# RWKV-7 main part of a hybrid decoder layer: the next group's inverse product and value transpose between the state steps, and finished projection blocks handled by kinds of operation behind the copies of px

## The chip, the cores and the metric

One core of one Trainium2 chip. The metric is device time in microseconds (us) of the whole program, lower is better. A profiled execution is told with two numbers: its time, and its span from the first to the last instruction of the program.

## The reference

One layer (sequence 1024, width 1024, fp32) of a trunk that mixes three heads groups in parallel (HGRN2, a dilated window attention, RWKV-7), followed by a gated MLP with a causal convolution, a per-layer embedding and a last norm. The change touches the RWKV-7 part alone, with 4 heads of 64 columns, and the input projection whose blocks are computed beside it:

```python
z = rmsnorm(h, norm_mix_g[l]) @ w_in[l]
a_q, a_f, a_i, a_g, b_q, b_k, b_v, c_in = jnp.split(z, splits, axis=-1)
...
def rwkv7_mix(c, ...):
    ...
    def step(state, inp):
        r_t, w_t, k_t, v_t, kk_t, a_t = inp
        sa = jnp.einsum('bhvk,bhk->bhv', state, -kk_t)
        state = (state * w_t[:, :, None, :] + sa[..., None] * (kk_t * a_t)[:, :, None, :]
                 + v_t[..., None] * k_t[:, :, None, :])
        return state, jnp.einsum('bhvk,bhk->bhv', state, r_t)
    _, y = lax.scan(step, s0, xs)
    mean = jnp.mean(y, axis=-1, keepdims=True)
    var = jnp.mean((y - mean) ** 2, axis=-1, keepdims=True)
    y = ((y - mean) * lax.rsqrt(var + RK_GN_EPS)).reshape(B_, S_, RK_WIDTH) * ln_w + ln_b
    ...
```

## The kernel before

The input projection has blocks of 128 columns by 1024 tokens. A block is 8 row tiles of `x`, each with three fp32r products (weight high part with `x` high and low, weight low part with `x` high; lines 130, 132, 134), for two halves of 512 tokens. Its sums lie in a PSUM tile `dp` of two banks; there are two such tiles. Four more banks are the pool `mx`, one bank to a tile, for everything else of the RWKV part.

RWKV runs over two head pairs, `p` = 0 and 1. For each pair: preparation, an inverse of 32x32 blocks on VectorE (DVE) with projection blocks on TensorE (PE) under it, and then the main part (`rwkv_groups`), which works through 16 chunks of 64 tokens in four groups of four. Here the order of PE, DVE, ScalarE (ACT) and GpSimd (POOL) is the order in which the program writes it (`manual_schedule`). SyncE (SP) and everything traced outside such a stretch is ordered by the planner of the framework, which puts instructions in by its own costs, between the written ones too. DMAs of weights and of finished blocks are issued from SP.

In the main part the projection is the filler: `fill(k)` issues k steps of a generator (`project_steps`), each step being the three products of one row tile and one half. A block has 16 steps, and three blocks are handed to each pair: 14, 15 and 24 to p=0, and 21, 22 and 27 to p=1. When the last step of a block is issued, its finishing is left in `self.pend["z"]`, and `self.pending("z")` issues it. Finishing (`project_done`, `finish`) multiplies the sums by the factor `R` of the norm, and by the kind of the block does more; the result `zst` goes to DRAM:

- kind 2: one DVE product with R out of PSUM (L470), nothing else
- kinds 0, 1 and 3: a scaling in place in PSUM on DVE (L306), a sigmoid on ACT (L473), and for 1 and 3 a DVE product of the two (L475)
- for kinds 0 to 2 of blocks under 24 the time axis is reversed, and the block is finished in two parts of 512

Block 14 is of kind 2, 15 of kind 3 (in one part of 1024), 21 of kind 1, 22, 24 and 27 of kind 2. The last projection blocks ahead of the main parts are 13 (kind 1) and 20 (kind 0).

One group before the change, in the written order (PE unless named; tile names as in the profile):

1. finish a waiting block; parts of the output norm of the first half (`rwkv_norm_in`, parts 0 and 3)
2. `pt` transposes of v; fill 1; inverse product `py` from `AB` and `T` (L860), ACT copy to `Y` (L861), POOL `scores_bd` of the next group (L801)
3. ACT places the v transposes into `XV` (L828, four copies); transposes of `ar`, placed into `Xr` (four copies); `sc` products (L871), masked by DVE into `AK` and `W` (L785); fill 1
4. `pu` from `U` and `Y` (L882), DVE `copy_predicated` into U (L883); transposes of bhat and khat (L821), placed by DVE into `PB` and by ACT into W; DVE `quad("T")` of the next group (L794); POOL copies into W; fill 1
5. `pk` (L896), ACT copy into Xr; fill 2; `px` (L901); ACT and DVE copies to `X` (L903), ACT copies to XV (L905); fill 2
6. `pgm` (L909), DVE adds into `GM` (L913, four instructions in two pairs); `pn` (L922), DVE `N`; weight split of the next block (`self.pending("w")`: ACT casts L106, POOL subtractions L108); fill 1
7. four state steps u = 0 to 3: `pS` from GM and S (L939), DVE `S` (L940), output products into `pyo` (L942, L944); a fill behind u = 0
8. DVE `quad("U")` of the next group; ACT copies pyo into y (L954, four copies)

A tile of the pool `mx` is taken again once all its readers are done.

Of the kernel before, what the change touches and what calls it, by code (L numbers as in the profile page):

```python
# [10 lines left out]
F32 = mybir.dt.float32  # L11
F32R = mybir.dt.float32r
U8 = mybir.dt.uint8
AF = mybir.ActivationFunctionType
ALU = mybir.AluOpType
# [3 lines left out]
P = 128  # L19
T = 1024  # L20
# [59 lines left out]
class Trunk:  # L80
# [375 lines left out]
    def project_done(self, j, ps):  # L456
        t = self.keep.tile([P, T], F32, tag="zst", name=self.nm("zst"), bufs=2)
        kind = (j - 8) % 4 if j < 24 else 2
        parts = [(t, ps, self.R)]
        if j < 24 and kind < 3:  # L460
            parts = [(t[:, :HT], ps[:, HT:][:, ::-1], self.R[:, HT:][:, ::-1]), (t[:, HT:], ps[:, :HT], self.R[:, :HT])]
        for part in parts:
            self.finish(kind, *part)
        d = self.zpool.tile([P, T], F32, tag=f"z{j}", name=f"z{j}")
        self.nc.sync.dma_start(d, t)
        self.z[j] = d
# [299 lines left out]
    def rwkv_groups(self, p, rp, d, y3, steps):  # L766

        nc, mxp = self.nc, self.mxp
        ar, v, gC = d["ar"], d["v"], d["gC"]
# [3 lines left out]
        def rt(name, shape, bufs=1):  # L773
            return rp.tile(shape, F32, tag=name, name=self.nm(name), bufs=bufs)

        def fill(k):
            for _ in range(k):
                next(steps)
# [8 lines left out]
        t = {}  # L787
# [11 lines left out]
        def scores_bd(g):  # L799
            t["AB", g] = w = rt("ABt", [P, 4, P])  # L800
            nc.gpsimd.tensor_tensor(w.rearrange("p u (h i) -> p u h i", i=64),  # L801
                                    d["sc"][:, group(g), :].unsqueeze(2).broadcast_to([P, 4, 2, 64]),
                                    msk[:, 0, :, :].unsqueeze(1).broadcast_to([P, 4, 2, 64]), ALU.mult)
# [14 lines left out]
        def turn(src):  # L818
            pt = mxp.tile([P, 2, P], F32, tag="mx", name=self.nm("pt"))
            for b in (0, 1):  # L820
                nc.tensor.transpose(pt[:, b, :], src(b), self.ident)  # L821
            return pt

        def place(pt, dst, copy, swap=0):
            for h, q in enumerate(Q):
                d4 = dst(h).rearrange("p (b two) v -> p b two v", two=2)
                for c in (0, 1):
                    copy(d4[Q[h ^ swap], :, c, :], pt[64 * c:64 * c + 64, :, q])  # L828
# [3 lines left out]
        W, XV = rt("W", [P, 4, 2, 2, 64]), rt("XV", [P, 4, 2, 64])  # L832
# [8 lines left out]
        quad("T", 0)  # L841
        quad("U", 0)
        add_ar(0)
        S = None
        for g in range(4):
            cs, last = group(g), g == 3
            c2 = lambda b: slice(4 * g + 2 * b, 4 * g + 2 * b + 2)
            t2 = lambda b: slice(256 * g + P * b, 256 * g + P * b + P)
            Xr = rt("xr", [P, 4, P])
            self.pending("z")  # L850
            if g == 2:
                self.rwkv_norm_in(p, d, 0, (0,))
            if last:
                self.rwkv_norm_in(p, d, 0, (3,))
            pv = turn(lambda b: v[:, t2(b)])
            fill(1)
            Y = rt("Y", [P, 4, P])
            py = mxp.tile([P, 4, P], F32, tag="mx", name=self.nm("py"))
            for u in range(4):
                nc.tensor.matmul(py[:, u, :], t["AB", g][:, u, :], t["T", g][:, u, :], start=True, stop=True)  # L860
            nc.scalar.copy(Y, py)  # L861
            if not last:
                scores_bd(g + 1)
            place(pv, lambda h: XV[:, :, h, :], nc.scalar.copy, 1)
            place(turn(lambda b: ar[:, c2(b), 0, :].rearrange("p c i -> p (c i)")), lambda h: Xr[:, :, 0:64], nc.scalar.copy)
            if g == 2:
                self.rwkv_norm_in(p, d, 0, (1,))
            ps = mxp.tile([P, 4, 2, 64], F32, tag="mx", name=self.nm("sc"))
            kbf = t["kb"].rearrange("p c a b -> p c (a b)")
            for u in range(4):  # L870
# [8 lines left out]
            U = t["U", g]  # L879
# [6 lines left out]
                quad("T", g + 1)  # L886
            for h, q in enumerate(Q):
                nc.gpsimd.tensor_copy(W[q, :, h, :, :], PB[q])
            if g == 2:
                self.rwkv_norm_in(p, d, 0, (2,))  # L890
            place(turn(lambda b: d["kh"][:, t2(b)]), lambda h: W[:, :, h, 1, :], nc.scalar.copy, 1)
            fill(1)
            pk = mxp.tile([P, 4, 64], F32, tag="mx", name=self.nm("pk"))
            for u in range(4):
# [8 lines left out]
                copy(X[q, :, q], px[q, :, 0:64])  # L903
            for h, q in enumerate(Q):
                nc.scalar.copy(XV[q, :, h, :], px[q, :, 64:128])  # L905
            fill(2)
            pg = mxp.tile([P, 4, 2, 64], F32, tag="mx", name=self.nm("pgm"))
            for u in range(4):
# [20 lines left out]
            py = mxp.tile([P, 4, 64], F32, tag="mx", name=self.nm("pyo"))  # L929
            for u in range(4):  # L930
# [14 lines left out]
                S = Sn  # L945
                if u == 0:
                    fill(1)
            if not last:
                quad("U", g + 1)
            y4 = y3.rearrange("p (b h) v -> p b h v", h=2)  # L950
            py4 = py.rearrange("p (b two) v -> p b two v", two=2)
            for h in (0, 1):
                for c in (0, 1):
                    nc.scalar.copy(y4[64 * c:64 * c + 64, 2 * g:2 * g + 2, h, :], py4[64 * h:64 * h + 64, :, c, :])  # L954


    def hgrn_setup(self):
# [938 lines left out]
```

## Time and profile before

| what | us |
|---|---|
| median of 3 runs | 1458.14 (1458.09 to 1458.71) |
| profiled execution | 1458.02 |
| its span | 1456.2 |
| PE busy in the span | 1427.3 |
| DVE, ACT, POOL busy | 1102.3, 635.3, 447.3 |
| main part of p=0 (four groups) | 146.28 to 215.13 |
| main part of p=1 (four groups) | 334.30 to 403.39 |

The times in a row of the timeline are the start and the length in us, then engine, line of the kernel, operation, output and inputs, and in brackets the idle time of the engine just before and what ended it. Rows of several equal instructions are merged (x2, x4). PEld is the weight load of PE, which overlaps its products. An fp32 product is two passes and counts twice.

### The profile page before, as it was taken

The page shows a single profiled execution, that of the slowest core. Times are in us where ns is not written, and L with a number is a line of the kernel's source. Part 1 is how long each engine was busy: PE and PEld are TensorE (multiplying, and loading weights), DVE is VectorE, ACT ScalarE, POOL GpSimd, SP SyncE. Part 2 cuts the span into 40 slices and gives each one's busy share as a digit, 9 for nine tenths or more (in the row PEclk, how much of TensorE's full clock was granted, in tenths as well). Part 3 has the DMA queues.
Part 4 walks back from the last instruction along what each step waited for, and adds up shares of the span by engine and source line. Part 5 has one row for each costly group of instructions (what it writes and reads, how often), then busy time and mean ns, then how long its engine had stood idle before and what let it go on. Part 6 is the DMA issues. An engine that isn't in the chain of part 4 may idle for free.

```text
span 1456.2 us, 20345 instructions
## 1 busy us (share of the span) xinstructions
PE 1427.3 (98%) x7480; PEld 1174.8 (81%) x7480; DVE 1102.3 (76%) x1672; ACT 635.3 (44%) x1131; POOL 447.3 (31%) x364
## 2 busy tenths in 40 slices
PE   9999999999999999899999999999999999999996
PEld 7888887888877777788878888888888888888885
DVE  6567565684677689637798889888888799777685
ACT  6531443213434565335544434444444444455552
POOL 2332342223421132222145545544454000002342
PEclk9999999999999999999999999999999999999998
DMA  5224021240151320165423332333333883352443
GB/s 215 69 82 114 30 74 58 66 129 31 58 203 44 116 73 23 66 224 209 153 93 109 109 100 96 109 103 107 108 96 122 311 287 96 103 165 58 127 157 115
DMA packets 80019, 167.84 MB, mean 115 GB/s; under 512 B 20080, under 2 KB 22256, under 8 KB 79920
## 3 DMA queue, kind: packets, MB, share of 16 engines
q1 hardware_dynamic: 65568, 145.44, 30.2%
q10 hardware_dynamic: 13408, 17.57, 3.6%
q0 software_dynamic: 944, 3.54, 0.7%
q8 instruction: 59, 0.97, 0.3%
q14 instruction: 40, 0.33, 0.1%
HBM read 120.12 MB, written 46.40 MB: 114 GB/s over the span
## 4 chain that ended last, share of the span: by engine, by line
PE 85%; DVE 6%; issue 3%; ACT 2%; POOL 2%; DMA 2%; SPq 0%; DVEq 0%; ACTq 0%; POOLq 0%
PE bg L1351 15%; PE bv L1351 11%; PE dp L130 8%; PE dp L134 8%; PE dp L132 8%; PE bg L1669 7%; PE bv L1669 7%; PE hsc L1029 2%; PE bv L130 1%; PE bv L134 1%; PE bv L132 1%; PE bg L130 1%; PE bg L132 1%; PE bg L134 1%; PE swq L1186 1%
## 5 line engine op out<-in xcount | busy, mean ns | idle before, releaser
L130 PE MATMUL dp<-xh,whi 128*128 128x512 f32 x544 | 197.5, 408 | 1.3 <-ACT xh L375 1.3
L134 PE MATMUL dp<-xh,wlo 128*128 128x512 f32 x544 | 189.1, 393 | 0.1
L132 PE MATMUL dp<-xl,whi 128*128 128x512 f32 x544 | 188.5, 392 | 0.4 <-DVE xl L376 0.3
L108 POOL TENSOR_TENSOR wlo<-raw,whi 128x512 fp32r<-128x512 f32 x84 | 136.4, 1643 | 75.1 <-ACT whi L106 75.1
L108 POOL TENSOR_TENSOR wlo<-wraw,whi 128x512 fp32r<-128x512 f32 x63 | 89.3, 1422 | 226.8 <-ACT whi L106 208.2
L1351 PE MATMUL bg<-t,whi 128*128 128x512 f32 x352 | 132.5, 389 | 0.8 <-DVE ct L1554 0.8
L106 ACT CAST whi<-wraw 128x512 fp32r<-128x512 f32 x120 | 72.6, 617 | 129.8 <-PE dp L132 87.0
L130 PEld LDWEIGHTS dp<-xh,whi 128*128 128x128 f32 x544 | 101.6, 189 | 24.0 <-issue 3.5
L134 PEld LDWEIGHTS dp<-xh,wlo 128*128 128x128 f32 x544 | 102.3, 188 | 22.3 <-POOL wlo L108 0.5
L132 PEld LDWEIGHTS dp<-xl,whi 128*128 128x128 f32 x544 | 102.4, 189 | 20.4 <-DVE xl L376 0.6
L108 POOL TENSOR_TENSOR wlo<-s,whi 128x512 fp32r<-128x512 f32 x44 | 66.6, 1514 | 160.9 <-ACT whi L106 160.9
L1669 PE MATMUL bg<-t,whi 128*128 128x512 f32 x308 | 94.9, 389 | 0.0
L1669 PE MATMUL bv<-t,whi 128*128 128x512 f32 x308 | 94.8, 389 | 0.0
L106 ACT CAST whi<-s 128x512 fp32r<-128x512 f32 x66 | 39.0, 620 | 122.3 <-PE bg L1351 113.4
L106 ACT CAST whi<-raw 128x512 fp32r<-128x512 f32 x88 | 52.7, 619 | 90.9 <-issue 48.3
L175 POOL TENSOR_TENSOR rst<-rst,mhalf 128x4 f32<-128x4 f32 (+1 forms) x9 | 10.1, 1130 | 222.7 <-DVE rst L173 222.7
L108 DVE TENSOR_TENSOR wlo<-wraw,whi 128x512 fp32r<-128x512 f32 x57 | 47.7, 836 | 40.2 <-ACT whi L106 35.8
L1351 PEld LDWEIGHTS bg<-t,whi 128*128 128x128 f32 x352 | 66.0, 188 | 14.7 <-ACT whi L106 1.1
L1665 ACT CAST t<-t 128x512 fp32r<-128x512 f32 x77 | 47.8, 623 | 47.6 <-PE bv L1669 34.1
L1669 PEld LDWEIGHTS bv<-t,whi 128*128 128x128 f32 x308 | 57.8, 188 | 12.0
L1669 PEld LDWEIGHTS bg<-t,whi 128*128 128x128 f32 x308 | 57.7, 188 | 12.0
L1351 PE MATMUL bg<-t,wlo 128*128 128x512 f32 x176 | 67.2, 389 | 0.0
(424 smaller groups left out, 3610.6 us busy)
## 6 DMA issues: line engine op xcount, KB each, us to landing
raw<-in_ffn_up_dram SPq DMA_DIRECT2D x44, 512.0 KB, 3.7
wraw<-in_w_in_dram SPq DMA_DIRECT2D x29, 512.0 KB, 3.7
z<-zst SPq DMA_DIRECT2D x18, 512.0 KB, 2.8
gb<-ct SPq DMA_DIRECT2D x33, 256.0 KB, 2.3
t<-gb SPq DMA_DIRECT2D x33, 256.0 KB, 2.8
t<-gt SPq DMA_DIRECT2D x33, 256.0 KB, 2.7
zl<-z SPq DMA_DIRECT2D x16, 512.0 KB, 4.1
wraw<-in_ple_gate_dram SPq DMA_DIRECT2D x16, 512.0 KB, 3.6
```

The lines of the kernel that those rows point to most:

```text
L106: nc.scalar.copy(hi, src)
L108: eng.tensor_tensor(lo, src, hi.bitcast(F32), ALU.subtract)
L130: nc.tensor.matmul(ps[hf], wh, xh[hf], start=first, stop=False)
L132: nc.tensor.matmul(ps[hf], wh, xl[hf], start=False, stop=False)
L134: nc.tensor.matmul(ps[hf], wl, xh[hf], start=False, stop=last)
L175: nc.gpsimd.tensor_tensor(r2[:, :n], r[:, :n], self.mhalf[:, :n], ALU.pow)
L1029: nc.tensor.matmul(sc[:, c, :], ks[:, c * P:(c + 1) * P], view(qt, c * P, [2 * n, 64 // n], [HT + n, 2], [1, n]), start=True, stop=True)
L1186: nc.tensor.matmul(pq[h][:, b:b + w], d["q"][hs, qb * P:nk], d["k"][hs, b:b + w], start=True, stop=True)
L1351: nc.tensor.matmul(ps, w[part == 2][:, s], X[k][part == 1], start=start and k == part == 0, stop=k == 3 and part == 2, skip_group_check=no ...
L1665: nc.scalar.copy(xh, x)
L1669: nc.tensor.matmul(ps[m], wt[part == 2][:, m * P:(m + 1) * P], (xh, xl)[part == 1], start=k == part == 0, stop=k == NK - 1 and part == 2)
```

## The change

Three edits. In `project_done` blocks of kinds 0, 1 and 3 are finished operation by operation over their parts instead of part by part. In the main part the inverse product with its copy to Y, `scores_bd` and `quad("U")` of the next group move behind state step 1, and the v transposes of the next group with a fill behind step 2; those of the first group stand ahead of the loop. The copies of pyo into y move into the next group, behind the placing of `ar`; finishing a block moves behind the copies of px; the parts of the norm move with them (0 into group 2 behind the placing of khat, 1 behind the copies of px, 2 into group 3, 3 behind step 1 of group 3, with a fill).

```diff
         if j < 24 and kind < 3:
             parts = [(t[:, :HT], ps[:, HT:][:, ::-1], self.R[:, HT:][:, ::-1]), (t[:, HT:], ps[:, :HT], self.R[:, :HT])]
-        for part in parts:
-            self.finish(kind, *part)
+        if kind == 2:
+            for part in parts:
+                self.finish(kind, *part)
+        else:
+            for _, src, r in parts:
+                self.scale(src, r)
+            for dst, src, _ in parts:
+                self.nc.scalar.activation(dst, src, AF.Sigmoid)
+            if kind in (1, 3):
+                for dst, src, _ in parts:
+                    self.nc.vector.tensor_tensor(dst, dst, src, ALU.mult)
...
-        S = None
+        def inverse_first(g):
+            t["Y"] = rt("Y", [P, 4, P])
+            py = mxp.tile([P, 4, P], F32, tag="mx", name=self.nm("py"))
+            for u in range(4):
+                nc.tensor.matmul(py[:, u, :], t["AB", g][:, u, :], t["T", g][:, u, :], start=True, stop=True)
+            nc.scalar.copy(t["Y"], py)
+            if g < 3:
+                scores_bd(g + 1)
+        def values_turn(g):
+            t["pv"] = turn(lambda b: v[:, 256 * g + P * b:256 * g + P * b + P])
+        def result(g, py):
...
+        S, before = None, None
+        values_turn(0)
+        fill(1)
+        inverse_first(0)
         for g in range(4):
...
-            Xr = rt("xr", [P, 4, P])
-            self.pending("z")
-            if g == 2:
-                self.rwkv_norm_in(p, d, 0, (0,))
-            if last:
-                self.rwkv_norm_in(p, d, 0, (3,))
-            pv = turn(lambda b: v[:, t2(b)])
-            fill(1)
-            Y = rt("Y", [P, 4, P])
-            py = mxp.tile([P, 4, P], F32, tag="mx", name=self.nm("py"))
...
-            place(pv, lambda h: XV[:, :, h, :], nc.scalar.copy, 1)
+            Xr, Y = rt("xr", [P, 4, P]), t["Y"]
+            place(t["pv"], lambda h: XV[:, :, h, :], nc.scalar.copy, 1)
             place(turn(lambda b: ar[:, c2(b), 0, :].rearrange("p c i -> p (c i)")), lambda h: Xr[:, :, 0:64], nc.scalar.copy)
-            if g == 2:
-                self.rwkv_norm_in(p, d, 0, (1,))
+            if before:
+                result(*before)
...
-            if g == 2:
+            if g == 3:
                 self.rwkv_norm_in(p, d, 0, (2,))
             place(turn(lambda b: d["kh"][:, t2(b)]), lambda h: W[:, :, h, 1, :], nc.scalar.copy, 1)
+            if g == 2:
+                self.rwkv_norm_in(p, d, 0, (0,))
             fill(1)
...
                 nc.scalar.copy(XV[q, :, h, :], px[q, :, 64:128])
+            if g == 2:
+                self.rwkv_norm_in(p, d, 0, (1,))
+            self.pending("z")
             fill(2)
...
                 if u == 0:
                     fill(1)
-            if not last:
-                quad("U", g + 1)
...
+                if u == 1:
+                    if last:
+                        self.rwkv_norm_in(p, d, 0, (3,))
+                        fill(1)
+                    else:
+                        inverse_first(g + 1)
+                        quad("U", g + 1)
+                if u == 2 and not last:
+                    values_turn(g + 1)
+                    fill(1)
+            before = g, py
+        result(*before)
```

More of the change, by code (lines that the diff above doesn't have):

```diff
@@ L843, in rwkv_groups @@
         add_ar(0)
-        S = None
+        def inverse_first(g):
[9 more added lines that the diff above has]
+        def result(g, py):
+            y4 = y3.rearrange("p (b h) v -> p b h v", h=2)
+            py4 = py.rearrange("p (b two) v -> p b two v", two=2)
+            for h in (0, 1):
+                for c in (0, 1):
+                    nc.scalar.copy(y4[64 * c:64 * c + 64, 2 * g:2 * g + 2, h, :], py4[64 * h:64 * h + 64, :, c, :])
+        S, before = None, None
+        values_turn(0)
+        fill(1)
+        inverse_first(0)
         for g in range(4):
@@ L848, in rwkv_groups @@
             t2 = lambda b: slice(256 * g + P * b, 256 * g + P * b + P)
-            Xr = rt("xr", [P, 4, P])
-            self.pending("z")
-            if g == 2:
-                self.rwkv_norm_in(p, d, 0, (0,))
-            if last:
-                self.rwkv_norm_in(p, d, 0, (3,))
-            pv = turn(lambda b: v[:, t2(b)])
-            fill(1)
-            Y = rt("Y", [P, 4, P])
-            py = mxp.tile([P, 4, P], F32, tag="mx", name=self.nm("py"))
-            for u in range(4):
-                nc.tensor.matmul(py[:, u, :], t["AB", g][:, u, :], t["T", g][:, u, :], start=True, stop=True)
-            nc.scalar.copy(Y, py)
-            if not last:
-                scores_bd(g + 1)
-            place(pv, lambda h: XV[:, :, h, :], nc.scalar.copy, 1)
+            Xr, Y = rt("xr", [P, 4, P]), t["Y"]
+            place(t["pv"], lambda h: XV[:, :, h, :], nc.scalar.copy, 1)
             place(turn(lambda b: ar[:, c2(b), 0, :].rearrange("p c i -> p (c i)")), lambda h: Xr[:, :, 0:64], nc.scalar.copy)
-            if g == 2:
-                self.rwkv_norm_in(p, d, 0, (1,))
+            if before:
+                result(*before)
             ps = mxp.tile([P, 4, 2, 64], F32, tag="mx", name=self.nm("sc"))
@@ L947, in rwkv_groups @@
                     fill(1)
-            if not last:
-                quad("U", g + 1)
[L950 to L954, printed above, removed]
+                if u == 1:
[10 more added lines that the diff above has]
+        result(*before)
     def hgrn_setup(self):
```

## The prediction

> **What bounds the kernel now.** The page first: TensorE (PE) is busy nearly all of the span, so time can only come from places where it waits or is fed badly.
>
> ```profile
> span 1456.2 us, 20345 instructions
> PE 1427.3 (98%) x7480; PEld 1174.8 (81%) x7480; DVE 1102.3 (76%) x1672; ACT 635.3 (44%) x1131; POOL 447.3 (31%) x364
> ```
>
> Next the view by stretches, cut at the transposes of v, one stretch for each group: the sum over the four groups of the first head pair (p=0), then the second and third group of the second pair (p=1). After the length stand PE, PEld, DVE, ACT and POOL busy, then the granted clock, the DMA share and GB/s.
>
> ```profile
> sum 68.85, PE 68.24 PEld 57.46 DVE 42.56 ACT 30.93 POOL 28.22; mean PE 17.06 PEld 14.37 DVE 10.64 ACT 7.73 POOL 7.05
> ...
> 351.30:368.11 16.81, 16.77 (x141) 14.31 (x141) 8.03 (x21) 6.21 (x21) 5.58 (x9) 1.00 0.11 32
> 368.11:386.80 18.69, 17.26 (x141) 14.26 (x141) 13.21 (x29) 10.11 (x28) 9.89 (x12) 1.00 0.07 29
> ```
>
> A group takes some 17 us (68.85 for four); the third of p=1 takes 18.69, 1.88 more than the one before it. What the change can win lies inside these eight groups. The granted clock is 1.00. Third view, the timeline of the third group of p=1, where a finished projection block (kind 1) sits ahead of the group's own work on ACT:
>
> ```profile
> 369.47 0.60 ACT L473 ACTIVATE zst<-dp 128x512 f32<-128x512 f32 x1
> 370.10 0.69 DVE L475 TENSOR_TENSOR zst<-zst,dp 128x512 f32<-128x512 f32 x1 [0.92 <-ACT zst L473]
> 371.55 0.60 ACT L473 ACTIVATE zst<-dp 128x512 f32<-128x512 f32 x1 [1.49 <-DVE dp L306]
> 372.68 1.16 PE L882 MATMUL pu<-U,Y 128*128 128x128 f32 x8 [0.77 <-ACT Y L861]
> 373.81 0.44 PE L821 MATMUL pt<-cst,bhat 128*128 128x128 f32 x2
> 374.91 0.44 PE L821 MATMUL pt<-cst,khat 128*128 128x128 f32 x2 [0.66 <-ACT xr L828]
> ```
>
> The sigmoid stands 1.49 us for the second scaling, which itself stands behind the first product on DVE. ACT's copies of Y, XV and xr come behind it, and PE waits for Y (at pu) and for xr (at the khat transpose). An ordinary group (second of p=1) for comparison:
>
> ```profile
> 353.11 0.38 PE L821 MATMUL pt<-cst,ar 128*128 128x128 f32 x2
> 353.33 1.06 PE L871 MATMUL sc<-ar,kbd 128*128 128x128 f32 x8
> 355.82 0.38 PE L821 MATMUL pt<-cst,bhat 128*128 128x128 f32 x2
> 356.24 0.44 PE L821 MATMUL pt<-cst,khat 128*128 128x128 f32 x2
> 360.94 0.43 DVE L903 COPY X<-px 64x256 f32<-64x256 f32 x1 [2.37 <-ACT X L903]
> 361.40 0.76 ACT L905 COPY XV<-px 64x256 f32<-64x256 f32 x2 [0.49 <-DVE X L903]
> 362.83 0.86 DVE L913 TENSOR_TENSOR GM<-pgm,addend 64x256 f32<-64x256 f32 x2 [1.46 <-PE pgm L909]
> 364.06 0.33 PE L939 MATMUL pS<-S,GM 128*128 128x64 f32 x2
> 364.83 0.48 PE L130 MATMUL dp<-xh,whi 128*128 128x512 f32 x1
> 366.41 0.39 PE L939 MATMUL pS<-S,GM 128*128 128x64 f32 x2
> 366.83 0.28 DVE L940 SCALAR_TENSOR_TENSOR S<-pS,gC,N 128x64 f32<-128x64 f32 x1 [0.57 <-PE pS L939]
> 367.26 0.39 PE L939 MATMUL pS<-S,GM 128*128 128x64 f32 x2
> ```
>
> **What the change wins.** (1) The khat transpose starts 0.42 us after that of bhat, where ar to sc, the same transposes unhindered, takes 0.22: it needs the PSUM buffer that ACT frees with the copies into xr. After the change Y is copied a step earlier and the v transpose is ready, so ACT opens the group with XV (1.1 us) and xr (1.1), done about 2.15 us after the ar transpose; khat is due at 2.85. The four result copies (1.1) come behind, done at 3.25 before pk at 4.0. So 0.20 goes in five groups, and 0.88 in the third of p=1 (373.81 to 374.91 against 0.22): 1.9 us. The pyo buffer now lives into the next group; the buffers of v, ar and sc come free in the order in which pu, bhat and khat need them, so I charge nothing (if khat got pyo's: 0.4 in each of six groups, 2.4).
>
> (2) The late Y of p=1: the group's excess of 1.88 less the 0.68 already in khat: 1.2 us. With Y a step early, nothing replaces it here.
>
> (3) State steps. One followed directly by the next takes 0.85 (366.41 to 367.26), one followed by a block product 0.77 (364.06 to 364.83): 0.08 each. The change puts the inverse product (0.9 us) behind step 1 and transpose with a fill behind step 2. Thirteen such joints make 1.1. In the third group of p=0 one joint is worse, 1.05 instead of 0.77:
>
> ```profile
> 195.44 0.39 PE L939 MATMUL pS<-S,GM 128*128 128x64 f32 x2
> ...
> 196.49 0.43 PE L939 MATMUL pS<-S,GM 128*128 128x64 f32 x2
> ```
>
> With that, 0.3 more (its S stood behind a weight subtraction on DVE): 1.4 us. The inverse products, the transposes and the fills only move: PE's own time for them is the same (37 fills inside instead of 36, one fewer behind, 0.69 us that is not lost). The joint costs of the new neighbours are unseen: plus or minus 0.03 each, zero taken.
>
> Here reading the share of busy time would mislead: busy leaves 0.04 of 16.81 in the second group of p=1, 1.43 in the third and 0.61 in all of p=0, so only about 2.1 could be won there, not 4.5, and the sum below would end at 1459.4. I take the starts, since (3) shows 0.08 lost between instructions that both count as busy. [...]
>
> **What it costs.** (4) The finishing now stands, in written order, between the copies of px and GM. DVE is free there from 361.37 to 362.83, 1.46 us. Kind 2 is two products with R of 0.7 or less and fits (first block of p=0, second of p=1): nothing. The first block of p=1 is kind 1. On the ordinary group's clock: scalings 361.4 to 362.8; sigmoids 362.8 to 364.0, ACT being done with XV at 362.2 and with the square of the norm (0.63) at 362.8; products 363.4 to 364.8; GM then takes 0.86, and step 0 starts at 365.7 instead of 364.06. Behind the waiting products on DVE stand GM, N and the S of every step, and PE waits for GM with all that follows it. Cost 1.7 us.
>
> (5) The second block of p=0 is kind 3, one part of 1024, so by kinds or not it is a chain:
>
> ```profile
> 205.71 1.23 DVE L306 TENSOR_TENSOR dp<-dp,rstd 128x1024 f32<-128x1024 f32 x1 [0.32 <-PE dp L134]
> 206.97 1.03 ACT L473 ACTIVATE zst<-dp 128x1024 f32<-128x1024 f32 x1
> 207.05 0.43 DVE L903 COPY X<-px 64x256 f32<-64x256 f32 x1
> 208.03 1.22 DVE L475 TENSOR_TENSOR zst<-zst,dp 128x1024 f32<-128x1024 f32 x1 [0.55 <-ACT zst L473]
> 209.17 0.85 DVE L913 TENSOR_TENSOR GM<-pgm,addend 64x256 f32<-64x256 f32 x2
> 210.17 0.40 PE L130 MATMUL dp<-xh,whi 128*128 128x512 f32 x1
> 210.41 0.33 PE L939 MATMUL pS<-S,GM 128*128 128x64 f32 x2
> ```
>
> Today the planner starts it ahead of the X copy and nobody waits. Afterwards it starts at 207.48: 1.23 + 1.03 + 1.22 with handovers ends at 211.0, GM 0.85 later, step 0 at 211.9 instead of 210.2: 1.7 us. A product of the next head pair (210.17) shows that PE's order is filled from outside in this group; the finished block's buffer frees at 211.0, so up to 0.86 of it can be filled. Between 0.85 and 1.7 I take 1.3.
>
> (6) The first groups keep their order, but the last block before them is now finished by kinds, outside the written order:
>
> ```profile
> 335.86 0.70 DVE L306 TENSOR_TENSOR dp<-dp,rstd 128x512 f32<-128x512 f32 x1 [0.66 <-ACT zst L473]
> 339.68 0.44 PE L821 MATMUL pt<-cst,khat 128*128 128x128 f32 x2 [0.49 <-ACT xr L828]
> ```
>
> The second scaling waited for the first sigmoid, so the halves of dp count as overlapping. Then the first sigmoid must now wait for both scalings, 0.7 later; ACT had 0.47 idle ahead of Y, so xr and khat slip by some 0.25 in each first group: 0.5 us. If the halves don't hold each other, 0.35 is won twice; the bounds are -0.7 and +0.8.
>
> (7) The rest. Mean and subtraction of the norm move into the 2.37 us for which DVE waits ahead of X: two operations of 128x512, some 0.7 each as in 370.10, and between them
>
> ```profile
> L728 DVE TENSOR_SCALAR gnm<-gnm x4: 171/172/1086, 182.6 to 405.5; 128x8 f32<-128x8 f32 x4
> ```
>
> so 1.6, at the worst 2.5: hidden, or 0.1 out. The variance pair goes to the same place one group on; the norm's last scaling and the U tile, some 0.7 each, behind step 1, with a product or fill between it and the next step. All hidden; without cover each would cost its own length. On POOL scores_bd goes ahead of the next group's key copies by more than a fill, and is needed a group later. On SP the z stores are issued up to most of a group later; a weight load of later blocks that stands behind one comes later too, and has the products of the block in hand to hide it. In the later stages the planner decides anew; its largest wait there bounds what a different draw is worth, 2.1 us either way, zero taken:
>
> ```profile
> PE hsc L1029 <- DVE qt L1034: 4.6, 4, 2.1
> ```
>
> **Sum.** Won 1.9 + 1.2 + 1.4 = 4.5; lost 1.7 + 1.3 + 0.5 = 3.5; net 1.0 us. The profiled execution took 1458.02 us (span 1456.2 and 1.82 around it), the median of the runs is 1458.14. 1458.02 - 1.0 = 1457.0. About 0.2%, 2.9 us, is what a measurement of this kernel can tell from no change.
>
> **Rivals.** *The stall ahead of GM doesn't come* (chance 0.25): sigmoids and products slip in beside pgm and pn, or fills cover them. Then 4.5 less 0.5: 1454.0 (1452.8 if the first groups win 0.7 too). For it speaks that today block two of p=0 costs nothing; against it that here the order is written and GM is behind the products on DVE.
>
> *Foreign casts stretch the chain; the slower side* (0.13). The planner puts weight splits of later blocks where ACT and DVE wait, and the new chain has such holes between scaling, sigmoid and product:
>
> ```profile
> 380.81 2.18 ACT L106 CAST whi<-wraw 128x512 fp32r<-128x512 f32 x4
> 385.72 1.40 DVE L108 TENSOR_TENSOR wlo<-wraw,whi 128x512 fp32r<-128x512 f32 x1
> ```
>
> Two casts (1.1) ahead of the sigmoids and one subtraction (1.4) ahead of the products add 2.5 in (4), and 1.7 in (5) where one cast can come: 4.2, 1461.2. It decides from 1.0 us of such stretching on.
>
> *The U tile holds a state step* (0.05). Behind step 1 it runs while POOL subtracts weights; it took up to 1.57 instead of 0.7:
>
> ```profile
> 387.24 1.57 DVE L794 TENSOR_TENSOR U<-Tc,cst 128x512 f32<-128x512 f32 x1
> 384.08 4.18 POOL L108 TENSOR_TENSOR wlo<-wraw,whi 128x512 fp32r<-128x512 f32 x3
> ```
>
> Step 1's S is there 0.7 us after its pS starts; U at 1.57 ends at 2.3, step 2's S at 2.6, and step 3 wants it at 3.4 (0.77 + 0.9, 0.77 + 0.15 + 0.78): covered. Only if U sat out two subtractions (1.4 each by the second row) and then took 0.7 would that S come at 4.5, 1.1 late, in the four groups that split weights: 4.4 us, 1461.4. [...]
>
> **How the numbers follow.** Forecast 0.57, rivals 0.25, 0.13, 0.05. Its own range is 1455.0 to 1459.2, from (5), (6) and part of the later draw. The whole range, 1453.4 to 1460.4, takes in most of the first rival and the beginning of the others. Faster by over 0.2% (under 1455.2): the first rival and a little of the forecast, 0.27; slower (over 1461.0): 0.11; the rest 0.62.
>
> **What would show it.** Right: khat 0.22 behind bhat from the second groups on; step to step never below a product; third group of p=1 near 18.1, waiting at pS for GM; fourth of p=0 waiting there too. Wrong: no wait at pS for GM (first rival), casts between scaling and sigmoid (second), a wait of pS for S (third), or main parts as forecast and a different loss behind 420 us.

## The result, and the profile after

The changed kernel takes 1461.38 us, median of 12 runs (1458.63 to 1463.67), against 1458.40 (12 runs, 1458.09 to 1460.26) for the kernel before on the same chip: a ratio of 1.0019, 95% interval 1.0011 to 1.0027. It is slower by about 3 us, where 1 us less was forecast. The profiled execution took 1461.37 us (span 1459.6 and 1.8 around it), 3.35 more than the one before.

The page of the changed kernel first. The head shows almost nothing: PE is busy 2.3 us more, at the same share.

```profile
span 1459.6 us, 20343 instructions
PE 1429.6 (98%) x7480; PEld 1177.3 (81%) x7480; DVE 1103.0 (76%) x1672; ACT 634.8 (43%) x1131; POOL 450.5 (31%) x364
```

That PE is *busier* by 2.3 us with the same 7480 instructions is itself the hint that instructions became longer, not only that PE waited. The waits of PE in the changed kernel (line waited at, who released it, us in total, times, longest):

```profile
PE pS L962 <- DVE GM L936: 2.0, 1, 2.0
...
PE dp L130 <- DVE zst L472: 0.9, 1, 0.9
```

The first row is the third group of p=1, the second the fourth group of p=0; in the main parts there is only one more, 0.7 us of the khat transpose in the first group of p=0. The wait at `pu` for Y, and the waits of the khat transpose in the later groups, are gone. The rest can't be seen there. It is in the view by stretches (length; busy time of PE, PEld, DVE, ACT and POOL; then the granted clock, the DMA share and GB/s). The first two rows are the second and third group of p=1, from one transpose of ar to the next; the others are cut to the edges of what they show:

```profile
353.37:370.00 16.63, 16.63 (x142) 14.26 (x141) 7.90 (x20) 6.23 (x22) 5.63 (x8) 1.00 0.08 30
370.00:390.81 20.81, 18.86 (x145) 15.75 (x145) 14.65 (x28) 10.41 (x31) 8.48 (x10) 0.92 0.17 54
380.61:384.02 3.41, 1.46 (x11) 0.99 (x10) 3.21 (x7) 2.14 (x5) 0.53 (x1) 1.00 0.35 143
384.02:387.43 3.41, 3.41 (x16) 2.89 (x16) 2.17 (x3) 0.00 (x0) 3.30 (x4) 0.50 0.03 11
387.43:390.84 3.41, 3.41 (x30) 2.84 (x29) 2.25 (x4) 1.40 (x5) 1.23 (x1) 1.00 0.63 168
493.25:496.66 3.41, 1.63 (x13) 1.11 (x12) 1.88 (x6) 3.40 (x7) 0.00 (x0) 1.00 0.97 332
496.66:500.07 3.41, 3.41 (x17) 3.41 (x18) 0.31 (x1) 0.78 (x2) 0.00 (x0) 0.50 0.87 348
```

An ordinary group got shorter (16.63; 16.81 before). The third group of p=1 got longer, and not by its wait alone: for 3.41 us behind the wait the granted clock is 0.50, and PE, busy all through, gets 16 instruction records done where the next 3.41 us have 30. The same happens at 496.66, far behind the change; the window ahead of it holds two waits of PE, 0.69 and 1.09 us long, which the kernel before has as well (0.7 and 1.09), there at full clock. In the kernel before the clock was below 1.00 only in the first 12 us and the last 11. The timeline of the changed kernel around the wait:

```profile
377.68 0.43 DVE L923 COPY X<-px 64x256 f32<-64x256 f32 x1 [0.69 <-ACT X L923]
...
378.14 1.43 DVE L306 TENSOR_TENSOR dp<-dp,rstd 128x512 f32<-128x512 f32 x2
...
379.60 1.09 ACT L469 ACTIVATE zst<-dp 128x512 f32<-128x512 f32 x2
...
380.00 0.50 PE L130 MATMUL dp<-xh,whi 128*128 128x512 f32 x1
...
380.58 2.17 ACT L106 CAST whi<-wraw 128x512 fp32r<-128x512 f32 x4
380.72 1.28 DVE L472 TENSOR_TENSOR zst<-zst,dp 128x512 f32<-128x512 f32 x2 [1.15 <-ACT zst L469]
381.93 0.85 DVE L936 TENSOR_TENSOR GM<-pgm,addend 64x256 f32<-64x256 f32 x2
...
382.92 0.41 PE L962 MATMUL pS<-S,GM 128*128 128x64 f32 x2 [1.95 <-DVE GM L936]
...
383.77 0.56 PE L130 MATMUL dp<-xh,whi 128*128 128x512 f32 x1
...
384.55 0.63 PE L134 MATMUL dp<-xh,wlo 128*128 128x512 f32 x1
384.98 0.52 PE L962 MATMUL pS<-S,GM 128*128 128x64 f32 x2
...
385.74 1.78 DVE L803 TENSOR_TENSOR U<-Tc,cst 128x512 f32<-128x512 f32 x1
...
386.33 1.64 PE L858 MATMUL py<-T,ABt 128*128 128x128 f32 x8
...
387.80 0.33 PE L962 MATMUL pS<-S,GM 128*128 128x64 f32 x2
```

Read down: scalings, both sigmoids, both products, and only then GM; PE stands at `pS` for 1.95 us. From the fill at 380.00 to `pS` go 2.92 us, where an ordinary group has 0.80: a cost of 2.12. Then the same instructions become long: a fill product of 0.63 instead of 0.40, the inverse product 1.64 instead of 1.11. Against the second group of p=1, where the clock is 1.00, the fill takes 1.21 us to the next `pS` (383.77 to 384.98) instead of 0.78, the state step 1.35 (to 386.33) instead of 0.79, and the inverse product 1.47 (to 387.80) instead of 0.95: together 1.5 us lost. By the groups it is 1.7 (from the transpose of ar at 370.00 to the next at 390.42 are 20.42 us, 16.63 in the second group, less the 2.12). I take 1.6, a cost that the prediction did not have.

**Theory.** The finishing ahead of GM makes a stall, as forecast; the stall makes PE's clock drop to half for a stretch behind it, and the length of those instructions is the second half of the price. **Rivals.** The halved stretch is chance, or comes from something else in the new order; or the loss is in the order between the state steps itself.

### The profile page after: what moved, and what is told of

It is laid out like the page before. It is cut to its first block, busy times and chain, and to the rows that moved or that the text cites. A ratio compares the mean times of both kernels' runs of the same rounds, so it can differ in the third digit from the quotient of the medians.

```text
span 1459.6 us, 20343 instructions
## 1 busy us (share of the span) xinstructions
PE 1429.6 (98%) x7480; PEld 1177.3 (81%) x7480; DVE 1103.0 (76%) x1672; ACT 634.8 (43%) x1131; POOL 450.5 (31%) x364
## 4 chain that ended last, share of the span: by engine, by line
PE 85%; DVE 6%; issue 3%; ACT 2%; DMA 2%; POOL 2%; SPq 0%; DVEq 0%; ACTq 0%; POOLq 0%
PE bg L1379 15%; PE bv L1379 11%; PE dp L130 8%; PE dp L134 8%; PE dp L132 8%; PE bg L1697 7%; PE bv L1697 7%; PE hsc L1057 1%; PE bv L130 1%; PE bv L134 1%; PE bv L132 1%; PE bg L130 1%; PE bg L134 1%; PE bg L132 1%; PE swq L1214 1%
```

## Experiments

All runs are in five rounds, beside the kernel before on the same chip. None leaves out any of the computation.

**Each part alone.** The first kernel is the one before with finishing by kinds of operation, at its old place. The second is the changed kernel with finishing part by part, at the head of the group.

```diff
 # kinds only (on the kernel before), in project_done
-        for part in parts:
-            self.finish(kind, *part)
+        if kind == 2: ...                  # scalings, then sigmoids, then products
 # main order only (on the changed kernel): project_done as before, and
+            self.pending("z")
             place(t["pv"], lambda h: XV[:, :, h, :], nc.scalar.copy, 1)
...
-            self.pending("z")
             fill(2)
```

> The kernel before with the first edit alone: blocks of kinds 0, 1 and 3 finished operation by operation over their parts; the main part stands as before. Theory A (the loss is the wait of step 0 for GM, and a stretch of halved clock that it brings): no such wait here, nothing halved that was not halved before; in the third group of p=1 the finishing stands at the head of the group as before, so pu and khat still wait, by a bit more or less; 1457.5 to 1459.0, the same as before. Theory B (the loss comes from the grouping by kinds itself, or from what the planner makes of the finished blocks outside the main parts): 1460 to 1461.5, as the changed kernel.

> The changed kernel with the finishing part by part again and at the head of the group, ahead of the placing of v; the inverse product, the v transposes and the result copies stay between the state steps. Theory A: GM is on time in the fourth group of p=0 and the third of p=1, pS waits for it no more. But in the third group of p=1 ACT does both sigmoids (the second behind the first product on DVE, about 2.7 us from the group's start) ahead of XV and xr, so xr ends near 4.9 us instead of 2.15 and khat, due at 2.85, waits 2 us: that stall takes the place of the other, with the same chance of a halved clock. 1459.5 to 1461.5. Theory B (grouping by kinds): without it the time falls to about 1455.5. Theory C (it is the interleaving of the state steps that costs): as theory A in time, but without a wait as long as 1.5 us anywhere in the main parts.

Kinds only: 1458.89 (11 runs), ratio 0.9996, interval 0.9987 to 1.0005, no change that can be told. Main order only: 1462.41 (11 runs), ratio 1.0019, interval 1.0011 to 1.0028, as slow as the whole change. Its timeline in the third group of p=1, and its stretches cut to the edges of the clock:

```profile
372.01 0.60 ACT L473 ACTIVATE zst<-dp 128x512 f32<-128x512 f32 x1 [1.49 <-DVE dp L306]
...
373.80 1.16 PE L892 MATMUL pu<-U,Y 128*128 128x128 f32 x8 [2.38 <-ACT XV L828]
```

```profile
372.58:375.99 3.41, 1.54 (x10) 1.17 (x10) 2.85 (x7) 3.15 (x13) 0.00 (x0) 1.00 0.37 154
375.99:379.40 3.41, 3.40 (x22) 2.54 (x23) 2.93 (x7) 1.37 (x5) 1.70 (x2) 0.50 0.00 0
```

Another wait, at another place (`pu` stands for the copies into XV, queued on ACT behind the second sigmoid; the expectation had put it at the khat transpose), and the same halved stretch behind it. So the halving is not tied to GM or to the new place of the finishing. And the two edits are no sum: with Y a step early, the old place of the finishing is worse than it was before.

**Take the stall away.** The finishing is cut in two: scalings and sigmoids behind the copies of px, products and the store behind state step 2. Once on the changed kernel, once on the order of the kernel before.

```diff
+        def rest():
             if kind in (1, 3):
                 for dst, src, _ in parts:
                     self.nc.vector.tensor_tensor(dst, dst, src, ALU.mult)
...
+        if later and kind in (1, 3):
+            self.pend["y"] = rest
+        else:
+            rest()
...
-            self.pending("z")
+            self.pending("z", later=True)
             fill(2)
...
+                if u == 2:
+                    self.pending("y")
```

> The changed kernel with the finishing cut in two: scalings and sigmoids stay behind the copies of px, the products of sigmoid and sum (kinds 1 and 3) and the store go behind state step 2. Theory A: the scalings fit into the 1.46 us that DVE has ahead of GM (two of 0.7, one of 1.23), so pS waits for GM by less than 0.3 us in both groups, no stretch around 384 us runs at half clock, and the time falls by the 2.1 us and the 0.9 us of these waits and 1.6 us of halved clock: 1456 to 1457.5, faster than before. Theory B or C: the waits go and the time stays at 1460 to 1461.5.

> The kernel before with the finishing grouped by kinds, its scalings and sigmoids behind the copies of px and its products behind state step 2, as in the two-stage version; the inverse product, the v transposes, the U tile, the norm and the result copies stay where they were before. If the interleaving with the state steps is worth only the khat waits (0.16 to 0.2 us in six groups, 1.1 us together) and the rest of the two-stage version's gain is the finishing that leaves the head of the third group of p=1 (1.9 us), then 0.9985 to 0.9993 of before, and the two-stage version stays ahead by 0.0005 to 0.001. If the interleaving is what won there: as before, 0.9995 to 1.0005. The wait of khat in ordinary groups stays at 0.42 from bhat, the state steps at 0.85 where they follow each other.

On the changed kernel: 1457.04 (11 runs, 1455.43 to 1457.59), ratio 0.9982, interval 0.9974 to 0.9991. On the order before: 1457.06 (11 runs), ratio 0.9986, interval 0.9978 to 0.9995. Both beat both kernels; the first stands 0.0037, some 5.4 us, below the changed kernel when each is taken against its own runs of before. The timeline of the first, same place:

```profile
376.79 1.43 DVE L306 TENSOR_TENSOR dp<-dp,rstd 128x512 f32<-128x512 f32 x2
...
378.26 0.86 DVE L943 TENSOR_TENSOR GM<-pgm,addend 64x256 f32<-64x256 f32 x2
378.26 1.09 ACT L469 ACTIVATE zst<-dp 128x512 f32<-128x512 f32 x2
...
379.46 0.33 PE L969 MATMUL pS<-S,GM 128*128 128x64 f32 x2
```

GM starts beside the sigmoids, 1.47 us behind the start of the scalings instead of 3.79, and `pS` has no wait. The two versions differ by the interleaving between the state steps; by their ratios that is worth 0.0004 (0.6 us), which their intervals don't tell from nothing.

**Keep the stall, fill PE.** Is the extra 1.6 us the stall's idleness? The changed kernel with eight products of 128x512 in the hole, written to the bank that `pS` then overwrites; then with four, and later with two. GM is as late as ever.

```diff
+                    if (p, g, u) == (1, 2, 0):
+                        wide = mxp.tile([P, HT], F32, tag="mx", name=self.nm("pS"))
+                        x = self.X[0][0][0]
+                        for _ in range(8):          # then range(4), range(2)
+                            nc.tensor.matmul(wide, x[:, :P], x, start=True, stop=True)
+                        pS = wide[:, :64]
...
```

> The changed kernel with eight additional products of 128x512 ahead of step 0 in the third group of p=1, whose sums are overwritten: they fill the time for which PE waited there (1.95 us by the trace, eight products at 0.23 are 1.85) and shorten no wait for GM. If the stall alone costs (plain theory A): GM comes as late as before, step 0 starts within 0.2 us of where it did, the time stays at 1461. If the idle stretch brings a halved clock besides: the stretch after 384 us runs at full clock, and the median falls by about 1.6 us to 1459.5 to 1460; the mean granted clock rises by about 0.001. If the halving has nothing to do with this wait: clock and time as in the changed kernel.

> The changed kernel with four additional products instead of eight ahead of step 0 in the third group of p=1, so that some 1.0 us of the 1.95 stays idle. If a halved stretch needs an idle time of well over 1 us: no halving behind it, 0.9997 to 1.0006 of before, as with eight products. If 1 us is enough: 1.0015 to 1.002, as the changed kernel. In between (1.0006 to 1.0015) if it comes in part of the runs.

> The changed kernel with two products of 128x512 in the hole instead of four: idle time of PE at pS about 1.4 us (1.95 without, 0.94 with four). Theory, sharpened from the profiles so far (the clock is judged in windows of 3.41 us on a fixed grid, and the next window is halved where PE is idle for more than about half of one, 1.6 to 1.8 us): no halved stretch behind this stall, wherever the grid lies, and a ratio near that with four, 1.0000 to 1.0008. Rival (any stall between 0.94 and 1.95 us can set it off, the bound lies nearer 1 us): a halved stretch within 4 us behind the stall, ratio 1.0011 to 1.0020. Rival (the grid doesn't matter, halving is chance in every window): halving in some profile or none, ratio between 1.0008 and 1.0016. In both theories the profile's other halved stretches lie whole multiples of 3.413 us from each other, and each follows a window with more than 1.6 us idle by the first one only.

Eight: 1459.07 (11 runs), ratio 1.0001, interval 0.9992 to 1.0009. Four: 1459.27 (11 runs), ratio 1.0003, interval 0.9994 to 1.0012. Two: 1462.22 (11 runs), ratio 1.0014, interval 1.0005 to 1.0023. The timeline with four, and the stretch behind the wait:

```profile
382.81 0.43 PE L969 MATMUL pS<-S,GM 128*128 128x64 f32 x2 [0.94 <-DVE GM L936]
```

```profile
384.00:388.00 4.00, 4.00 (x32) 3.19 (x30) 3.45 (x5) 0.84 (x2) 3.89 (x4) 1.00 0.02 9
```

and with two, where PE waits 1.40 us at `pS`, the window around the end of the wait and the two behind it:

```profile
381.95:385.36 3.41, 2.32 (x18) 1.86 (x19) 2.77 (x9) 1.01 (x2) 1.03 (x2) 1.00 0.37 154
385.36:388.78 3.42, 3.42 (x19) 3.19 (x20) 3.02 (x3) 0.59 (x1) 3.42 (x3) 0.50 0.06 11
388.78:392.19 3.41, 3.41 (x16) 2.89 (x17) 0.28 (x1) 0.97 (x4) 0.53 (x1) 0.50 0.73 240
```

With four, `pS` starts at 382.81 (382.92 in the changed kernel), so the wait for GM costs what it cost; only PE's idleness is cut, from 1.95 to 0.94 us. The clock stays at 1.00, at this place with eight products too (that profile, at 1462.51 the slowest of the eleven runs, has two halved stretches far behind, at 594.95 and 670.04), and the kernel is faster than the changed one by 0.0016 (0.0018 with eight), some 2.5 us. PE does *more* work in less time. With two the halved stretch is there, and most of the gain is gone. So the ratio follows the idleness that is left: 1.0001, 1.0003 (0.94 us), 1.0014 (1.40 us), 1.0019 (1.95 us), at the same lateness of GM. The intervals of neighbouring values overlap, those of eight products and of none do not. The granted clock that is listed with each run says the same: its mean is 0.9936 over the twelve runs of the changed kernel, 0.9940 with two products, 0.9954 with four and 0.9955 with eight. That shows that idleness makes the second half of the price. The sharpened expectation for two products, that only a window idle for more than about half its length sets the halving off, is refuted: 1.40 us of waiting did it, with 1.09 us of idleness in the window ahead of the halved one, and for two stretches at that. Of the rivals written there, the one with the bound between 0.94 and 1.40 us for such a stall stands. The ratio would also fit the third rival, that halving is chance in every window; against it, the starts of the two places in that profile, 385.36 and 596.99, are 62.0 times 3.413 us apart, where 3.413 is a 33rd of the 112.64 us between the two starts in the changed kernel. The halving doesn't come in every execution either: two of the eleven runs with two products, 1459.01 and 1459.24, have a mean clock of 0.997 and the others at most 0.994, and of the changed kernel's twelve the one at 1458.63 has 0.997.

The filling wins 2.5 and not the 1.6 us of one stretch. By the mean clocks that is still the clock: 0.0018 more of some 1460 us is 2.6 us, an estimate that takes PE as the limit all through. So the average run of the changed kernel loses more than its profile shows at this place, as the profile with two products does, which has two stretches there.

**A longer stall at the same place.** The changed kernel with finishing part by part, at the new place: the chain gets longer by what doing both scalings and both sigmoids together had saved.

```diff
 # in project_done of the changed kernel
-        if kind == 2: ...                  # scalings, then sigmoids, then products
+        for part in parts:
+            self.finish(kind, *part)
```

> The changed kernel with the first edit undone: the finishing stands behind the copies of px, but part by part. In the third group of p=1 DVE then does scaling, waits for the sigmoid, product, scaling, waits, product: 0.7 + 0.6 + 0.7 twice with handovers, 4.2 us instead of 3.5 ahead of GM. If the grouping shortens the stall: pS waits for GM by 2.6 to 2.9 us instead of 1.95, halved clock behind it as before or longer, 1.0023 to 1.0035 of before. If the grouping is without effect: 1.0019 as the changed kernel.

1463.56 (5 runs), ratio 1.0034, interval 1.0022 to 1.0046. PE waits 2.9 us at `pS`, and the halved clock lasts for two stretches:

```profile
382.96:386.37 3.41, 2.17 (x10) 1.87 (x11) 2.54 (x7) 1.67 (x4) 0.96 (x2) 0.50 0.37 154
386.37:389.78 3.41, 3.41 (x17) 2.98 (x16) 2.14 (x3) 0.00 (x0) 3.41 (x3) 0.50 0.15 25
```

The longer chain adds 1.0 us of waiting; by the ratios 2.2 us are added to the changed kernel's time, though the two intervals overlap.

**A stall with nothing else of the change.** The kernel before, with useless VectorE work ahead of GM in the second group of p=1, which is otherwise undisturbed. First on a new tile, then on the decay tile after its last reader.

```diff
 # behind the copies of px, in the kernel before
+            if (p, g) == (1, 1):
+                junk = rt("junk", [P, HT])
+                nc.vector.memset(junk, 0.0)
+                for _ in range(4):
+                    nc.vector.tensor_tensor(junk, junk, self.R[:, :HT], ALU.mult)
 # second kernel, instead
+                for _ in range(8):
+                    nc.vector.tensor_tensor(AK, AK, pm[:, 0, :].unsqueeze(1).broadcast_to([P, 4, 64]), ALU.mult)
```

> The kernel before with additional work on DVE in the second group of p=1, ahead of GM: a memset (0.5) and four products of 128x512 (0.7 each) on a tile that nobody reads, 3.25 us where 1.46 are free, so that pS waits for GM by about 1.8 us and nothing else changes. If such a wait costs its length: 1.0012 of before (plus 1.8 us). If it also brings a halved clock in most runs: 1.0018 to 1.0025, and a stretch of 3.4 us at half clock behind the wait in the trace, where the block products take about twice their time.

> The kernel before, with eight 64x512 products on VectorE more (the decay tile times a mask, written over the decay tile, which nothing reads any more there; nothing of the output changes) in the second group of pair 1 of the main part, ahead of the masking of S; no new tile, no other queue touched. Theory (a stall of about 2 us on TensorE costs its own length and then a stretch of halved clock that opens behind it): pS waits about 2 us for the masking there, the trace shows one stretch at 0.5 granted clock within some 4 us behind it, and the median lies 2.0 + 0.3 to 2.0 + 2 us above the kernel before, ratio 1.0016 to 1.0028. Rival (the stall costs only its length, and the clock's stretches in the changed kernel are chance): a wait of the same length, no halved stretch at that place, ratio 1.0010 to 1.0015. Rival (the changed kernel's loss is the finishing's and not the stall's): ratio below 1.0008.

The first gave 1469.11 (6 runs), ratio 1.0074, interval 1.0061 to 1.0088, and is inconclusive as a price: the new tile changed later stages too (a wait of 1.6 us at 1380.30 with a halved stretch from 1381.87, which the kernel before does not have). At the place meant, `pS` waits 2.54 us, and two halved stretches follow, from 368.11 to 374.94. The second: 1464.27 (5 runs), ratio 1.0043, interval 1.0029 to 1.0056. The eight operations took 4.46 us, 1.0 more than eight maskings of AK would (0.43 each), so the wait was longer than meant. Its timeline and its stretches:

```profile
361.45 4.46 DVE L908 TENSOR_TENSOR AKt<-AKt,pm 128x256 f32<-128x256 f32 x8
...
366.93 0.41 PE L942 MATMUL pS<-S,GM 128*128 128x64 f32 x2 [2.65 <-DVE GM L916]
```

```profile
365.25:368.66 3.41, 1.73 (x13) 1.48 (x13) 2.93 (x8) 0.00 (x0) 0.40 (x1) 1.00 0.00 0
368.66:372.07 3.41, 3.41 (x23) 2.83 (x21) 0.69 (x3) 0.00 (x0) 0.00 (x0) 0.50 0.00 0
372.07:375.48 3.41, 3.41 (x16) 3.00 (x15) 2.06 (x4) 1.64 (x5) 0.00 (x0) 0.50 0.00 0
```

The expected ratio (1.0016 to 1.0028) is missed on the high side, because the stall was 2.65 us and not 2.0 and was followed by two halved stretches. The kind of outcome is that of the theory: this kernel has neither the new order nor the new finishing, and the clock halves behind the stall. In place it costs 5.9 us: from the transpose of ar at 353.15 to the one at 375.85 are 22.70 us, against 353.11 to 369.93, 16.82, in the kernel before. That is 2.65 of waiting and 3.2 of slower work. In the profiled execution 1.2 of it comes back by the next stage, where the `hsc` products that began at 426.7 before begin at 431.4, 4.7 later: in the next group ACT and DVE catch up while PE is late, and the wait of 0.77 at `pu` is gone.

## Why the prediction was wrong, by its steps

Two steps failed. Step (3) counted a gain of 1.4 us that the new order doesn't have. And step (4) priced the stall ahead of GM by its length alone: the clock of 1.00 that the prediction read in the trace before was taken to stay, a term put at nothing without a reason, and it fell to 0.50 behind the stall. The stall itself came where it was forecast, and for the reason given.

Against its own net of -1.0, the profiled execution came out at +3.35. The starts of the same products in the two profiles show where. The first v transposes of p=1 are 0.97 later (335.27, before 334.30). Behind both main parts the first product `hpo` is 1.56 later (496.52, before 494.96), and behind the halved stretch at 496.66 `hsc` is 3.17 later (543.84, before 540.67); some 0.2 comes after that. So the main parts came out at +1.56 where -1.0 was forecast. The stretch at 496.66 is the draw of one execution: the waits ahead of it are not the change's.

- **(1) khat, won 1.9: right.** khat now starts 0.26 behind bhat in the second to fourth groups (356.08 and 356.34 in the second of p=1) instead of 0.42 and, in the third of p=1, 1.10. Five times 0.16 and 0.84: 1.6.
- **(2) late Y, won 1.2: right.** No wait at `pu` is left.
- **(3) joints of the state steps, won 1.4: wrong; it is about nothing.** I read the 0.08 between two state steps as something that goes when they are parted. Only the second of the two joints had it: step 1 to step 2 took 0.80 (365.61 to 366.41), step 2 to step 3 0.85. And most of it moved. The timeline of PE in the second group of p=1 before:

```profile
365.61 0.33 PE L939 MATMUL pS<-S,GM 128*128 128x64 f32 x2
...
369.04 1.05 PE L860 MATMUL py<-T,ABt 128*128 128x128 f32 x8
...
369.93 0.38 PE L821 MATMUL pt<-cst,ar 128*128 128x128 f32 x2
```

  and after the change:

```profile
364.18 0.33 PE L962 MATMUL pS<-S,GM 128*128 128x64 f32 x2
...
366.52 1.11 PE L858 MATMUL py<-T,ABt 128*128 128x128 f32 x8
367.47 0.33 PE L962 MATMUL pS<-S,GM 128*128 128x64 f32 x2
...
370.00 0.39 PE L830 MATMUL pt<-cst,ar 128*128 128x128 f32 x2
```

  From the first `pS` to the transpose of ar, with the same four steps, two fills, the v transposes and the inverse product in both kernels, are 5.82 us; before, 364.06 to 369.93, 5.87. The inverse product takes 0.95 to the next start instead of 0.89 (369.04 to 369.93 before). From ar to ar the group gains 0.19 (16.63 instead of 16.82): 0.14 ahead of the first `pS`, by khat, and 0.05 behind it, of the 0.16 forecast for its two joints. "The joint costs of the new neighbours are unseen: plus or minus 0.03 each, zero taken" is the sentence that failed: a difference between two neighbourhoods is no gain until the new neighbour has a row of its own.
- **(4) the stall ahead of GM, cost 1.7: mechanism right, sized 2.12, and its consequence missed.** The products start at 380.72, behind *both* sigmoids (379.60 for 1.09), not behind the first. That the halves of one tile count as overlapping I used in (6) and forgot here. The larger part of what was missed is the halved clock, 1.6 us. The trace before had no sign of it: its longest waits in the main parts are 0.77 and 0.66, and a longer one behind them, 2.11 us ahead of 593.58, is not followed by a halved clock there.
- **(5) the kind-3 block, cost 1.3: right, 1.1.** The timeline of the fourth group of p=0 after the change:

```profile
207.01 1.23 DVE L306 TENSOR_TENSOR dp<-dp,rstd 128x1024 f32<-128x1024 f32 x1
...
209.34 1.22 DVE L472 TENSOR_TENSOR zst<-zst,dp 128x1024 f32<-128x1024 f32 x1 [1.09 <-ACT zst L469]
...
210.71 0.70 PE L130 MATMUL dp<-xh,whi 128*128 128x512 f32 x2 [0.87 <-DVE zst L472]
...
211.71 0.33 PE L962 MATMUL pS<-S,GM 128*128 128x64 f32 x2
```

  The chain is the one written down, 0.5 earlier, and as forecast a product of the next head pair takes up a part: PE idles 0.87, then products that wait for the finished block's buffer run until GM is there. By the end of p=0 it is rather 1.2: 0.97 later there, less the 0.21 of (6), plus three times 0.16 of (1). That idle stretch trips no halving.
- **(6) first groups, cost 0.5: half right.** p=0 slipped by 0.21, as forecast. In p=1 ACT's copies into xr slipped too, by 0.2 against the group's start (339.71 for 1.08), but khat, at 340.02, no longer waits for them and came 0.63 sooner. Why it doesn't is not shown; that the gain of 0.4 lies inside the bounds given is luck.
- **(7) the rest at nothing: right for the named operations.** The norm's subtraction ends 0.69 ahead of the DVE copy of X. U took 1.78 beside POOL's subtractions, more than the 1.57 feared, and no state step waits for S behind it. What was drawn later is not a wait but a clock: at 496.66 the profiled execution loses another 1.6 us. That lies inside the 2.1 allowed, but not for the reason given.

The sum by these: won 1.6 + 1.2 + 0.4 = 3.2, lost 2.1 + 1.1 + 1.6 + 1.6 = 6.4, net +3.2 of the +3.35 measured. Without the two halved stretches it would be nothing, and there the kernels with four and eight filling products stand (1.0003, 1.0001), whose mean clocks of 0.9954 and 0.9955 are those of the kernel before. Over all runs, too, most of the loss is the clock's: 0.9936 in the changed kernel, 0.9952 to 0.9954 in the kernel before as it ran beside the experiments; the difference, 0.0016 to 0.0018 of some 1460 us, is an estimated 2.3 to 2.6 of the 3 us.

**The rivals.** "The stall ahead of GM doesn't come" did not happen. "Foreign casts stretch the chain", whose 1461.2 is by chance near the measured time, did not either: ACT's four casts (380.58) come as the sigmoids end. "The U tile holds a state step" neither. On the signs named: khat 0.26, near the 0.22 forecast, and waits were seen at both places named, in the fourth group of p=0 not at `pS` itself but at a product put in just ahead of it; "step to step never below a product" was seen and was worth nothing; "third group of p=1 near 18.1" was missed, it takes 20.4 (370.00 to 390.42), of which 1.6 by the clock.

## What to carry to other kernels

A stall on TensorE is to be priced at its length and at the slower clock that can follow it: here 1.95 us of idleness cost about 1.6 us more in the profile and 2.65 us cost 3.2 more, while a wait of 2.13 us (at 596.76 in the changed kernel) that lay across two windows was followed by none of it. So such a stall is to be avoided, or filled, with useless products if there are no others: in the profiles it was followed by full clock when filled to 0.94 us, and by half when filled to 1.40 us. Where a chain DVE, ACT, DVE stands ahead of something that PE waits for, cut it at its handovers and put the second half behind what is waited for, which here won 2 to 2.6 us against the kernel before, in either order. And a gap between two starts belongs to the pair of neighbours: when one of them is exchanged, look for the row of the new pair before counting it as won.

## What the runs showed of the hardware

- The granted clock was 0.50 in stretches of 3.41 us. In the changed kernel they begin at 384.02 and 496.66, 112.64 us or 33.0 times 3.413 apart. In all eight profiles with several such stretches behind the first 13 us and ahead of the last 20, their starts are whole numbers of 3.413 us apart (48.0 with kinds only, 62.0 with two products); the pieces of a profile counted off so from a halved stretch are its windows, and their edges its grid. One stretch followed a stall of 1.95 us (the changed kernel) and of 2.38 us (main order only); two of them, 6.82 us, followed 1.40, 2.54, 2.65 and 2.9 us; none followed 0.94, 0.87 or less in the main parts. In the changed kernel 1.95 us was enough, in a window in which PE was busy for 1.46 of 3.41 us.
- The same wait was followed by a halved stretch in one profile and by none in two others. It is the one of some 2.1 us near 592, far behind the change: in the kernel with kinds only it falls into one window (2.12 us idle), and the next window has a clock of 0.50; in the changed kernel it lies across two (1.01 and 1.12 us idle), as in the one before (2.11 us long), and the clock behind it stays at 1.00. The stretches of kinds only, then those of the changed kernel:

```profile
590.83:594.24 3.41, 1.29 (x8) 0.81 (x7) 2.73 (x3) 0.00 (x0) 1.19 (x2) 1.00 0.00 0
594.24:597.65 3.41, 3.41 (x28) 3.19 (x28) 1.30 (x2) 0.00 (x0) 0.00 (x0) 0.50 0.03 5
```

```profile
592.23:595.64 3.41, 2.40 (x12) 1.68 (x11) 2.88 (x5) 0.62 (x1) 2.03 (x2) 1.00 0.01 2
595.64:599.05 3.41, 2.29 (x30) 2.20 (x32) 2.10 (x4) 0.00 (x0) 0.00 (x0) 1.00 0.02 5
```

  With the 1.6 us lost at 384.02 for one stretch, runs of one kernel would by estimate differ by steps of some 1.6 us, and the twelve of the kernel before do lie in two clusters, 1458.1 to 1458.7 and 1459.7 to 1460.3. It fits the profiles, of which there is one for each kernel, and was not tried.
- In these profiles PE's idle time in one window went with the halving better than the length of a wait did. The halved stretches give the grid of eleven of the twelve profiles. Behind the first 13 us and ahead of the last 20, all eleven windows with 1.78 us or more of idle time were followed by a halved one, and three of the five with 1.60 to 1.73. Those with 1.53 or 1.54 us near 614 us, one in each of ten of these profiles, were not.
- What sets a halved stretch off stays open all the same. It is not PE's idle time in the window ahead alone: 1.09 us with two filling products was followed by halving, as was 0.97 ahead of 670.04 with eight, while 1.12 in the last row above was not; and in the last experiment the second stretch came although PE was busy all through the first.
- Eight VectorE operations of 128x256 one behind the other took 4.46 us, 0.56 each, against 0.43 for a single masking of the same size in the same group (AK, at 354.47, which reads the products `sc` and not AK itself). The cause was not tried.
